# The forward substitution of a chunked delta rule: 30 small instructions per group, on GpSimd or on VectorE

## The chip, the core and the metric

One core of a Trainium2 chip runs the whole program in one launch. The metric is the device time of that launch in microseconds (us), median of several runs, lower is better. Engines: PE is TensorE (matmuls; PEld its weight loads), DVE is VectorE, ACT is ScalarE, POOL is GpSimd, SP is SyncE, which here issues nearly all DMAs.

## The reference

One step of a hybrid encoder layer over 1024 prompt tokens and 64 sample tokens, model width 1024, float32. Adaptive modulation and an RMS norm, one input projection whose columns feed four head groups of width 256 (a depthwise convolution, a gated delta rule, pooling, and a stick-breaking attention), concatenation, one output projection, then modulation, norm and a SwiGLU feed-forward layer. The change is in the gated delta rule, which works on chunks of 64 tokens; in each chunk a unit lower triangular system of 64 equations is solved, and the state S is carried from chunk to chunk:

```python
lmat = jnp.where(strict, jnp.einsum('nbhid,nbhjd->nbhij', kb, kc) * decay, 0.0)
sol = lax.linalg.triangular_solve(lmat + jnp.eye(CHUNK), rhs, left_side=True, lower=True, unit_diagonal=True)
...
v_new = u_i - jnp.einsum('bhcd,bhde->bhce', w_i, S)
o = jnp.einsum('bhcd,bhde->bhce', q_i, S) + jnp.einsum('bhij,bhje->bhie', attn_i, v_new)
S = S * gl[..., None, None] + jnp.einsum('bhcd,bhce->bhde', k_i, v_new)
```

## The kernel before, in words

The tokens are two halves: HA has 512 prompt tokens, HB 512 prompt and the 64 sample tokens. Each half goes through input projection, the four head groups, output projection and feed-forward layer; work of the two halves overlaps.

**Order.** The program is written with tiles and a scheduler. The scheduler decides the order of the instructions on every engine, from data dependences, its own estimate of durations and priorities; `tc.high_priority()` raises the priority of what is issued inside it. Each engine then executes its own list strictly in that order, so an instruction that waits holds up all that stand behind it on its engine. A change in one place can therefore change the order of distant work.

**Weights.** Every projection splits a float32 weight tile of 128x1024 in two parts, `whi` and the remainder `wlo`, so that three matmuls give nearly float32 accuracy. `load_w` does it, at high priority: SP loads `wraw`, ACT makes `whi`, DVE makes `wlo` (L123), each in two buffers. PE multiplies (`pg`, L138) only as fast as DVE delivers `wlo`.

**The delta rule.** `delta(h)` calls `dn_group` five times: groups 1 and 2 for HA, 3 and 4 for HB's prompt tokens (four chunks and 64 partitions each), group 5 for the sample tokens (one chunk, 16 partitions, state `S_s`). A group makes `nl`, the negated triangular matrix. Its 16x16 diagonal blocks are inverted by forward substitution, with one block per partition, which takes a change of layout through DRAM:

1. `nl` goes to DRAM (`nld`, two DMAs) and comes back as `fsn` (four DMAs), one block of 256 numbers per partition.
2. `fst` is a copy of `fsn` with 1 added on its diagonal, then 14 times a multiply into `fsu` and an add into `fst`: 30 instructions, each depending on the one before.
3. `fst` goes to DRAM (`xd`, four DMAs) and comes back as `X` (two DMAs).
4. PE transposes `X` (`pw_...<-cst,X`, called pw0 below), ACT copies it to `Y`, and PE and DVE (`W`, `Y`, `X`) combine blocks twice; then `pu`, `pwt`, the state update (`pvn`, `vn`, `pkv`), the norm (`oss`) and `pof`, `kbe` to DRAM for the output projection.

**Modulation of the sample tokens.** `ada_sample` loads 32 tiles `wads` of 512 KB into two buffers by SP; DVE reduces each with one custom instruction (L212). The two buffers are shared with tiles (`mixs`) that HB's output projection needs. `wadt` is the same for the prompt tokens.

**HB's output projection** starts when `mixs` stands: `mixt` loaded from DRAM into two buffers, split by ACT and DVE. After it PE works through HB's feed-forward layer to the end.

Of the kernel before, what the change touches and what calls it, by code (L numbers as in the profile page):

```python
# [11 lines left out]
ALU = mybir.AluOpType  # L12
# [47 lines left out]
def hybrid_encoder_kernel(ctx: ExitStack, tc: tile.TileContext, io):  # L60
    nc = tc.nc
# [57 lines left out]
    def copy_v(out, in_):  # L119
        nc.vector.tensor_copy(out=out, in_=in_)  # L120

    def tt(out, a, b, op):
        nc.vector.tensor_tensor(out=out, in0=a, in1=b, op=op)  # L123
# [4 lines left out]
    def ts(out, a, s1, s2, op0, op1=None):  # L128
        if op1 is None:
            nc.vector.tensor_scalar(out, a, s1, None, op0)  # L130
        else:
            nc.vector.tensor_scalar(out, a, s1, s2, op0, op1)

    def ptt(out, a, b, op):
        nc.gpsimd.tensor_tensor(out=out, in0=a, in1=b, op=op)  # L135
# [551 lines left out]
    def dn_group(h, feats, gate, D, ch0, nch, tok0, mtok0, S):  # L687
# [4 lines left out]
        def T4(tag, bufs=1):  # L692
            return dn.tile([P, 576], F32, tag=tag, name=tag)[:, 0:128 * NCH]
# [42 lines left out]
        tmp = T4("X")  # L736
# [35 lines left out]
        nx = 2 * nch  # L772
# [3 lines left out]
        N = dn.tile([64, 256], F32, tag="fsn", name="fsn")[0:8 * nx]  # L776
        T = dn.tile([64, 256], F32, tag="fst", name="fst")[0:8 * nx]
        tmp = dn.tile([64, 64], F32, tag="fsu", name="fsu")[0:8 * nx]
        for q in range(4):
            nc.sync.dma_start(out=N[2 * nx * q:2 * nx * (q + 1)].rearrange("p (i j) -> p i j", j=16),  # L780
                              in_=ext[q, :, :, :, q].rearrange("i h x j -> (h x) i j"))
        N3, T3 = N.rearrange("p (i j) -> p i j", j=16), T.rearrange("p (i j) -> p i j", j=16)
        nc.gpsimd.tensor_copy(out=T, in_=N)
        nc.gpsimd.tensor_scalar(T[:, 0:256:17], T[:, 0:256:17], 1.0, None, ALU.add)
        for k in range(1, 15):
            n = 15 - k
            u3 = tmp[:, 0:n * k].rearrange("p (i j) -> p i j", j=k)
            ptt(u3, N3[:, k + 1:16, k:k + 1].to_broadcast([8 * nx, n, k]), T3[:, k:k + 1, 0:k].to_broadcast([8 * nx, n, k]), ALU.mult)
            ptt(T3[:, k + 1:16, 0:k], T3[:, k + 1:16, 0:k], u3, ALU.add)
        for q in range(4):  # L790
            nc.sync.dma_start(out=ins[q, :, :, :, q].rearrange("i h x j -> (h x) i j"),
                              in_=T[2 * nx * q:2 * nx * (q + 1)].rearrange("p (i j) -> p i j", j=16))
# [26 lines left out]
        for c in range(nch):  # L819
            pv2 = PS("pvn")  # L820
            for pair in range(2):
                j = (pair * nch + c) * 64
# [9 lines left out]
            for pair in range(2):  # L832
                j = (pair * nch + c) * 64
# [19 lines left out]
    def delta(h):  # L853
        D = dn_decays(h)
        for b in range(2):
            feats, gate = dn_feats(h, 256 * b, 256)
            for g in range(4 // NCH):
                dn_group(h, feats, gate, D, 4 * b + NCH * g, NCH, 64 * NCH * g, 256 * b + 64 * NCH * g, S_p)
        if h.samp:
            feats, gate = dn_feats(h, 512, 64)  # L860
            dn_group(h, feats, gate, D, 8, 1, 0, 512, S_s)
            nc.sync.dma_start(out=io["dn_s"], in_=S_s)
            nc.sync.dma_start(out=io["dn_p"], in_=S_p)
# [491 lines left out]
```

## Time and profile before

| | before |
|---|---|
| median of 3 runs (range) | 1495.17 us (1493.13 to 1499.02) |
| the profiled execution | 1496.6 us |
| its span in the trace | 1494.5 us |
| PE busy | 1406.4 us (94%) |
| DVE busy | 1026.7 us (69%) |
| ACT busy | 662.7 us (44%) |
| POOL busy | 88.5 us (6%) |
| mean granted TensorE clock | 0.971 |

The span is what the trace covers from the first to the last instruction; the execution is 2.1 us longer. Busy shares are means over the span, and stages differ much. A granted clock of 1 is 2.4 GHz, and half of it is 1.2 GHz.

### The profile page before, as it was taken

Reading aid. Unit: us, or ns where it says so; the run is one execution under the profiler, and the core shown is the slowest. Engines: PE = TensorE matmul, PEld = TensorE weight load, DVE = VectorE, ACT = ScalarE, POOL = GpSimd, SP = SyncE. Lnnn points to the kernel's source line nnn. Section 1 sums busy time; section 2 is a strip of 40 time slices with the busy share of each in tenths; the row PEclk is TensorE's granted clock in tenths of the full one; section 3 lists DMA queues with packets and bytes.
Section 4 is the critical chain, followed back from the end, with each engine's and each line's share of the span. In section 5 each row is a group of like instructions: output and inputs, shape, how many; then the busy total and the mean of one; then the engine's idle time right before and its main releaser. Section 6 shows DMA issues by size and latency. Waiting matters only on the chain.

```text
span 1494.5 us, 24787 instructions
## 1 busy us (share of the span) xinstructions
PE 1406.4 (94%) x9824; PEld 1222.5 (82%) x9824; DVE 1026.7 (69%) x1816; ACT 662.7 (44%) x1191; POOL 88.5 (6%) x196
## 2 busy tenths in 40 slices
PE   7999899979988799799999899999899999999999
PEld 5777688857966577587778587889799999999998
DVE  8788798855798999856765887444755545444444
ACT  4467554745474468556765332222422222222221
POOL 0003000300003000400210000000000000000000
PEclk9999999979998899899999899999999999999999
DMA  8675555555753422533324786222322222222222
GB/s 310 239 229 144 193 166 162 165 167 172 256 174 101 141 75 80 151 109 101 94 84 119 246 285 210 99 85 85 113 99 81 80 81 85 85 86 85 86 79 98
DMA packets 106867, 205.42 MB, mean 137 GB/s; under 512 B 39360, under 2 KB 49024, under 8 KB 106752
## 3 DMA queue, kind: packets, MB, share of 16 engines
q1 hardware_dynamic: 99936, 193.36, 39.9%
q0 software_dynamic: 6816, 10.49, 3.1%
q8 instruction: 77, 1.26, 0.3%
q14 instruction: 38, 0.31, 0.1%
HBM read 175.57 MB, written 28.24 MB: 136 GB/s over the span
## 4 chain that ended last, share of the span: by engine, by line
PE 65%; DMA 13%; DVE 12%; issue 4%; POOL 3%; ACT 2%; SPq 1%; DVEq 0%; POOLq 0%; ACTq 0%
PE pg L138 55%; DMA wadt<-in_wadat_dram 3%; DMA wads<-in_wadat_dram 3%; DVE cy L126 2%; DVE wlo L123 2%; PE pk L138 2%; PE psC L141 1%; POOL fst L135 1%; POOL fsu L135 1%; DVE lo L126 1%; PE psO L141 1%; PE z L141 1%; DVE wads L212 1%; ACT whi L117 1%; DMA wraw<-in_wup_dram 1%
## 5 line engine op out<-in xcount | busy, mean ns | idle before, releaser
L138 PE MATMUL pg<-hi,whi 128*128 128x288 f32 (+1 forms) x1504 | 506.0, 337 | 13.7 <-ACT hi L114 5.0
L138 PE MATMUL pg<-hi,wlo 128*128 128x288 f32 (+1 forms) x1504 | 500.4, 333 | 6.6 <-DVE wlo L123 6.6
L138 PE MATMUL pg<-lo,whi 128*128 128x288 f32 (+1 forms) x1504 | 499.3, 333 | 2.2 <-DVE lo L126 1.6
L117 ACT ACTIVATE whi<-wraw 128x1024 fp32r<-128x1024 f32 (+2 forms) x192 | 199.6, 1041 | 475.5 <-PE pg L138 411.4
L138 PEld LDWEIGHTS pg<-hi,whi 128*128 128x128 f32 x1504 | 286.5, 191 | 43.3 <-ACT whi L117 6.2
L138 PEld LDWEIGHTS pg<-hi,wlo 128*128 128x128 f32 x1504 | 286.2, 190 | 33.2 <-DVE wlo L123 9.0
L138 PEld LDWEIGHTS pg<-lo,whi 128*128 128x128 f32 x1504 | 287.0, 191 | 27.7 <-issue 2.9
L123 DVE TENSOR_TENSOR wlo<-wraw,whi 128x1024 fp32r<-128x1024 f32 (+2 forms) x192 | 230.4, 1200 | 104.9 <-ACT whi L117 103.0
L138 PE MATMUL pg<-g,whi 128*128 128x288 f32 (+1 forms) x1056 | 252.0, 330 | 1.4 <-DVE xA L126 0.9
L138 PEld LDWEIGHTS pg<-g,whi 128*128 128x128 f32 x1056 | 177.4, 188 | 18.3 <-DVE xA L126 2.2
L138 PE MATMUL pg<-g,wlo 128*128 128x288 f32 (+1 forms) x528 | 171.8, 328 | 0.0
L126 DVE SCALAR_TENSOR_TENSOR xs<-pg,mod,xs 128x288 f32<-128x288 f32 (+2 forms) x288 | 106.5, 412 | 85.7 <-PE pg L138 82.5
L123 DVE TENSOR_TENSOR fa<-fa,pg 128x288 f32<-128x288 f32 (+1 forms) x66 | 35.0, 531 | 106.6 <-PE pg L138 102.9
L138 PEld LDWEIGHTS pg<-g,wlo 128*128 128x128 f32 x528 | 99.3, 188 | 7.4
L126 DVE SCALAR_TENSOR_TENSOR cy<-cvb,vec,cy 128x512 f32<-128x512 f32 (+1 forms) x120 | 93.4, 793 | 0.3
L126 DVE SCALAR_TENSOR_TENSOR xA<-pg,mod,xA 128x512 f32<-128x512 f32 x96 | 70.6, 746 | 22.1 <-PE pg L138 21.6
L212 DVE CUSTOM_DVE_ANT_0 wadt<-wadt,cb,vec 128x1024 f32<-128x1024 f32 x32 | 41.0, 1282 | 31.1 <-DMA wadt<-in_wadat_dram 31.0
L114 ACT ACTIVATE e<-e 128x512 f32<-128x512 f32 (+4 forms) x100 | 52.0, 520 | 0.7
L138 PE MATMUL pg<-mixs,whi 128*128 128x288 f32 x256 | 50.9, 295 | 0.0
L212 DVE CUSTOM_DVE_ANT_0 wads<-wads,cb,vec 128x1024 f32<-128x1024 f32 x32 | 40.9, 1281 | 11.1 <-DMA wads<-in_wadat_dram 11.0
L114 ACT ACTIVATE zs<-zs 128x512 f32<-128x512 f32 (+4 forms) x50 | 25.9, 517 | 47.3 <-DVE zs L123 47.2
L138 PEld LDWEIGHTS pg<-mixs,whi 128*128 128x128 f32 x256 | 41.0, 188 | 0.1
(296 smaller groups left out, 1811.2 us busy)
## 6 DMA issues: line engine op xcount, KB each, us to landing
wraw<-in_wgate_dram SPq DMA_DIRECT2D x44, 512.0 KB, 3.3
wraw<-in_wup_dram SPq DMA_DIRECT2D x44, 512.0 KB, 3.3
wraw<-in_wdown_dram SPq DMA_DIRECT2D x44, 512.0 KB, 3.3
wadt<-in_wadat_dram SPq DMA_DIRECT2D x32, 512.0 KB, 5.0
wads<-in_wadat_dram SPq DMA_DIRECT2D x32, 512.0 KB, 4.4
wraw<-in_wfm_dram SPq DMA_DIRECT2D x30, 512.0 KB, 3.6
wraw<-in_wout_dram SPq DMA_DIRECT2D x16, 512.0 KB, 3.8
xA<-in_xa_dram SPq DMA_DIRECT2D x16, 256.0 KB, 6.0
```

Of the source, the lines that this page charges most:

```text
L114: nc.scalar.activation(out, in_, func, bias=bias, scale=scale)
L117: nc.scalar.activation(out, in_, ACTF.Copy)
L123: nc.vector.tensor_tensor(out=out, in0=a, in1=b, op=op)
L126: nc.vector.scalar_tensor_tensor(out, a, s, b, op0, op1)
L135: nc.gpsimd.tensor_tensor(out=out, in0=a, in1=b, op=op)
L138: return nc.tensor.matmul(out, lhsT=lhsT, rhs=rhs, start=start, stop=stop)
L141: nc.tensor.matmul(out, lhsT=lhsT, rhs=rhs, start=start, stop=stop, skip_group_check=True)
L212: nc.vector.tensor_tensor_reduce(out=junk, in0=w, in1=cbt[g], scale=1.0, scalar=V("b_ada", col), op0=ALU.mult, op1=ALU.add, accum_out=mod[ ...
```

## The change

The copy, the added diagonal and the 28 steps of each of the five groups are issued to DVE instead of POOL, inside `tc.high_priority()`. Shapes, data and the DMAs around them are the same.

```diff
-        nc.gpsimd.tensor_copy(out=T, in_=N)
-        nc.gpsimd.tensor_scalar(T[:, 0:256:17], T[:, 0:256:17], 1.0, None, ALU.add)
-        for k in range(1, 15):
-            n = 15 - k
-            u3 = tmp[:, 0:n * k].rearrange("p (i j) -> p i j", j=k)
-            ptt(u3, N3[:, k + 1:16, k:k + 1].to_broadcast([8 * nx, n, k]), T3[:, k:k + 1, 0:k].to_broadcast([8 * nx, n, k]), ALU.mult)
-            ptt(T3[:, k + 1:16, 0:k], T3[:, k + 1:16, 0:k], u3, ALU.add)
+        with tc.high_priority():
+            copy_v(T, N)
+            ts(T[:, 0:256:17], T[:, 0:256:17], 1.0, None, ALU.add)
+            for k in range(1, 15):
+                n = 15 - k
+                u3 = tmp[:, 0:n * k].rearrange("p (i j) -> p i j", j=k)
+                tt(u3, N3[:, k + 1:16, k:k + 1].to_broadcast([8 * nx, n, k]), T3[:, k:k + 1, 0:k].to_broadcast([8 * nx, n, k]), ALU.mult)
+                tt(T3[:, k + 1:16, 0:k], T3[:, k + 1:16, 0:k], u3, ALU.add)
```

`ptt` is POOL's tensor-tensor instruction, `tt`, `ts` and `copy_v` are DVE's. What the scheduler makes of it is read from the order of instructions on the engines.

First, POOL in group 1 before, where steps of the substitution stand alone (the other groups read alike):

```order
L135 TENSOR_TENSOR fsu<-fsn,fst 64x26
L135 TENSOR_TENSOR fst<-fst,fsu 64x13x2
L135 TENSOR_TENSOR fsu<-fsn,fst 64x36
L135 TENSOR_TENSOR fst<-fst,fsu 64x12x3
L135 TENSOR_TENSOR fsu<-fsn,fst 64x44
L135 TENSOR_TENSOR fst<-fst,fsu 64x11x4
```

And DVE in group 3 now, where `dnf`, `dne` belong to the delta rule's features, `zs`, `sl`, `pl` to the attention and `cy` to the convolution:

```order
L123 TENSOR_TENSOR dnf_4852<-dnf_4852,dne 128x512
L123 TENSOR_TENSOR sl<-e,sh 128x384
L123 TENSOR_TENSOR pl<-zs,ph 128x256
L126 SCALAR_TENSOR_TENSOR dne<-dnf_4874,dne 128x512
L123 TENSOR_TENSOR fst<-fst,fsu 64x13x2
L123 TENSOR_TENSOR zs<-zs,psC 128x384
L123 TENSOR_TENSOR fsu<-fsn,fst 64x36
L123 TENSOR_TENSOR fst<-fst,fsu 64x12x3
L123 TENSOR_TENSOR fsu<-fsn,fst 64x44
L123 TENSOR_TENSOR cy_6720<-cy_6720,cvr 128x606
L123 TENSOR_TENSOR cy_6769<-cy_6769,cvr 128x606
L123 TENSOR_TENSOR fst<-fst,fsu 64x11x4
```

The steps moved to DVE, and they do not stand together there: between the first and the last of a group's 30 rows DVE has other rows, most in group 3, where there are 96.

Second, PE where group 5's `X` is used. Before, matmuls of the feed-forward layer (`pg`) and of the attention (`psC`, `z`) stand around pw0:

```order
L138 MATMUL pg<-hi_7283,whi 128x512
L138 MATMUL pg<-lo_7284,whi 128x512
L138 MATMUL pw_5497<-cst,X 64x64
L138 MATMUL pg<-hi_7283,wlo 128x512
L138 MATMUL pw_5497<-cst,X 64x64 x3
L141 MATMUL psC<-sl,u_r 128x512
L141 MATMUL z<-q_6266,k_6264 128x512 x2
```

Now the same place reads:

```order
L138 MATMUL pg<-g_8821,wlo 128x512
L138 MATMUL pw_5497<-cst,X 64x64 x4
L138 MATMUL pw<-Y,nl 64x64 x4
L138 MATMUL py<-W,X 64x64 x4
L138 MATMUL px<-X,W 64x64 x4
L138 MATMUL pw<-Y,nl 64x64 x4
L138 MATMUL py<-W,X 64x64 x4
L138 MATMUL pu<-vb,Y 64x64 x4
L138 MATMUL pwt<-Y,kbe 64x64 x4
L138 MATMUL pvn<-S_s,X 64x64
```

The group's matmuls moved next to each other, down to its `pof` (not shown), and behind work of HA's feed-forward layer that stood after them before.

Third, DVE at the same place. Before, the blocks are combined between other rows, and no `wads` row stands near:

```order
L123 TENSOR_TENSOR pl<-zs,ph 128x512
L123 TENSOR_TENSOR W<-pw,cst 128x128
L126 SCALAR_TENSOR_TENSOR fe<-fa,fe 128x512
L123 TENSOR_TENSOR sl<-e,sh 128x512
L123 TENSOR_TENSOR fa<-fa,fe 128x512
L123 TENSOR_TENSOR fa<-fa,pg 128x512
L123 TENSOR_TENSOR wlo<-wraw,whi 128x1024
L123 TENSOR_TENSOR Y<-Y,py 128x128
L123 TENSOR_TENSOR X<-X,px 128x128
```

Now the last rows of the substitution stand behind the last rows of `wads`, and the combination follows at once:

```order
L123 TENSOR_TENSOR fst<-fst,fsu 16x2x13
L212 ISA wads,mod<-wads,cb_154,vec 128x1024
L212 ISA mod 128x1
L123 TENSOR_TENSOR fsu<-fsn,fst 16x14
L123 TENSOR_TENSOR fst<-fst,fsu 16x14
L123 TENSOR_TENSOR W<-pw,cst 128x128
L123 TENSOR_TENSOR Y<-Y,py 128x128
L123 TENSOR_TENSOR X<-X,px 128x128
```

All 32 `wads` rows moved ahead of group 5's last step; before, the first of them stood behind group 5's `kbe`.

## Rows read from the trace of the kernel before

**Rows 1.** The page: engines, and DVE's busy tenths in 40 slices

```profile
PE 1406.4 (94%) x9824; PEld 1222.5 (82%) x9824; DVE 1026.7 (69%) x1816; ACT 662.7 (44%) x1191; POOL 88.5 (6%) x196
...
DVE  8788798855798999856765887444755545444444
```

**Rows 2.** Waits of PE: for what, us in total, times, longest

```profile
PE pw L138 <- DMA X<-xd: 26.8, 4, 9.7
PE pg L138 <- DVE wlo L123: 6.6, 7, 2.0
```

**Rows 3.** Timeline of PE, pw0 of groups 1 to 5, and matmuls after group 1's

```profile
156.53 0.30 PE L138 MATMUL pw<-cst,X 64*64 64x64 f32 x2 [2.97 <-DMA X<-xd]
...
160.62 0.63 PE L138 MATMUL pg<-hi,whi 128*128 128x512 f32 x1
...
161.43 0.39 PE L138 MATMUL pg<-hi,wlo 128*128 128x512 f32 x1
...
307.65 0.44 PE L138 MATMUL pw<-cst,X 64*64 64x64 f32 x2 [9.67 <-DMA X<-xd]
...
472.57 0.45 PE L138 MATMUL pw<-cst,X 64*64 64x64 f32 x2 [6.66 <-DMA X<-xd]
...
631.62 0.44 PE L138 MATMUL pw<-cst,X 64*64 64x64 f32 x2 [7.50 <-DMA X<-xd]
...
756.16 0.33 PE L138 MATMUL pw<-cst,X 64*64 64x64 f32 x2
```

**Rows 4.** Busy time by stretch: PE, PEld, DVE, ACT, POOL; then granted clock

```profile
0.00:400.00 400.00, 364.87 (x2858) 304.67 (x2859) 307.13 (x592) 219.01 (x444) 34.91 (x82) 0.96 0.63 198
400.00:627.00 227.00, 195.99 (x1379) 149.46 (x1377) 218.11 (x371) 144.09 (x270) 34.19 (x70) 0.95 0.43 128
627.00:740.00 113.00, 107.87 (x842) 86.01 (x843) 73.03 (x128) 69.72 (x145) 6.86 (x13) 0.96 0.34 103
...
819.00:925.00 106.00, 97.28 (x395) 75.86 (x395) 90.76 (x137) 36.14 (x55) 0.00 (x0) 0.94 0.78 256
925.00:1494.00 569.00, 561.35 (x3926) 543.67 (x3924) 288.96 (x518) 144.60 (x195) 0.00 (x0) 0.99 0.27 89
```

**Rows 5.** POOL's timeline, first and last row of group 1, last of group 5

```profile
134.57 0.79 POOL L783 COPY fst<-fsn 64x256 f32<-64x256 f32 x1
...
148.60 0.21 POOL L135 TENSOR_TENSOR fst<-fst,fsu 64x14 f32<-64x14 f32 x1
...
750.18 0.21 POOL L135 TENSOR_TENSOR fst<-fst,fsu 16x14 f32<-16x14 f32 x1
```

**Rows 6.** DVE's groups: shape and count, busy us and mean ns of one, idle before

```profile
L123 DVE TENSOR_TENSOR wlo<-wraw,whi 128x1024 fp32r<-128x1024 f32 x178 | 217.4, 1222 | 102.2 <-ACT whi L117 100.3 <-PE pl L138 0.5
L126 DVE SCALAR_TENSOR_TENSOR cy<-cvb,vec,cy 128x606 f32<-128x606 f32 x60 | 49.7, 842 | 0.0
L212 DVE CUSTOM_DVE_ANT_0 wads<-wads,cb,vec 128x1024 f32<-128x1024 f32 x32 | 40.9, 1281 | 11.1 <-DMA wads<-in_wadat_dram 11.0
L123 DVE TENSOR_TENSOR cvb<-cvb,cve 128x64 f32<-128x64 f32 x2 | 0.4, 216 | 0.0
L123 DVE TENSOR_TENSOR plo<-plo,plb 64x16 f32<-64x16 f32 x4 | 0.7, 167 | 0.1
L123 DVE TENSOR_TENSOR W<-pw,cst 128x128 f32<-128x128 f32 x2 | 0.6, 292 | 2.7 <-PE pw L138 2.7
```

**Rows 7.** DVE's timeline: two wlo, the first and the last wads

```profile
535.42 1.22 DVE L123 TENSOR_TENSOR wlo<-wraw,whi 128x1024 fp32r<-128x1024 f32 x1
...
737.63 1.22 DVE L123 TENSOR_TENSOR wlo<-wraw,whi 128x1024 fp32r<-128x1024 f32 x1
...
823.02 1.28 DVE L212 CUSTOM_DVE_ANT_0 wads<-wads,cb,vec 128x1024 f32<-128x1024 f32 x1
...
921.52 1.28 DVE L212 CUSTOM_DVE_ANT_0 wads<-wads,cb,vec 128x1024 f32<-128x1024 f32 x1
```

**Rows 8.** PE's timeline in group 5: one small batch of matmuls

```profile
762.07 0.45 PE L138 MATMUL pw<-Y,nl 64*64 64x64 f32 x8
```

## The prediction

> **What bounds the kernel now.** I read the page first. PE is busy 1406.4 of 1494.5 us, DVE 1026.7 and POOL only 88.5, but DVE's slices are uneven: eights and nines in the first half, fours and fives at the end [rows 1]. So I cut the span into stretches [rows 4]. From 400 to 627 us DVE is busy 218.1 of 227 us while PE has 31 us idle: DVE bounds there. After 925 us PE is busy 561 of 569 us: PE bounds to the end. Between them DVE has slack, except from 819 to 925 us, where the `wads` tiles pass (DVE 90.8 of 106 us, PE 97.3, clock 0.94).
>
> The waits of PE show what the chain of the delta rule costs: 26.8 us in four waits for `X` [rows 2]. The timeline gives them: 2.97, 9.67, 6.66 and 7.50 us in groups 1 to 4, none in group 5 [rows 3]. After each the clock is at half for some us: behind group 1's wait a 128x512 matmul takes 0.63 us at 160.62 and 0.39 from 161.43, four to five us after PE resumed [rows 3]. Taking 4 to 7 us at the halved level, 2 to 3.5 us lost each, the four waits cost about 10 us more.
>
> POOL needs 14.2 us for group 1, from 134.57 to 148.81 [rows 5]. In group 5 the last step ends at 750.39 [rows 5] and pw0 starts at 756.16 [rows 3]: 5.8 us for the way through DRAM, which the change leaves alone.
>
> **The change, part by part.** *The steps' own price.* DVE had no such instruction; the nearest rows are 0.167 us for 64x16 and 0.216 us for 128x64 [rows 6], and the steps have 14 to 56 numbers per partition, so 30 of them take 5.0 to 6.5 us, 25 to 32 us in five groups. Done in one piece they would save 8 to 9 us of the chain in each group. But the order shows that they are not in one piece. Between the first and last of group 3's rows stand 96 others, and pricing all rows between copy and last step with the mean of their form (1.22 for `wlo`, 0.84 for a `cy` row, 1.28 for `wads` [rows 6] and so on) gives 20, 45, 65, 30 and 44 us for the five groups, against 14.2 on POOL in group 1. The chain gets longer, and the scheduler has pushed pw0 back by 12 to 88 us of PE work to suit. What that does I work out in four terms, by what PE has lost (time less the full-clock price of the rows that PE has executed) at four places.
>
> *Term 1, up to the third gate tile of HA's feed-forward layer.* Its `wlo` starts at 535.4 us [rows 7]. Summing the orders by mean durations, DVE's rows up to it take 445.7 us before and 484.5 now: the steps of groups 1, 2 and most of 3, and attention, convolution and state rows that now come before it. PE's rows before its use take 360.1 and 361.4. Before, PE had lost 535.4 - 360.1 = 175.3 us there, and DVE had stood idle 89.7. Of DVE's idle time the waits for `X` in groups 1 and 2 go (12.6 us and 4 of clock): their pw0 now stands behind a `wlo` that DVE makes about when the last step is done. I leave 3 us for what remains. That gives 484.5 + 89.7 - 16.6 + 3 = 560.6 at the tile, and PE has lost 560.6 - 361.4 = 199: **+24 us**. Bounds: +10, if DVE finds other gaps filled, and +32, if each of three groups also holds DVE for 3 us at the copy, which waits for its four DMAs with `wlo` rows queued behind it.
>
> *Term 2, from there to a feed-forward tile at 737.6 us* [rows 7]. Before, PE's rows up to it sum to 528.8, so it had lost 208.8: 33.5 us in this part, of which 10 to DVE until 627, 10.5 to group 4's wait for `X` and its clock, 13 to smaller things. Now DVE's lead over PE's needs has come back: by 627 us its lag, rows of DVE less rows of PE, has fallen from 123 at the gate tile to 103. So the first goes, group 4's wait shrinks to 3 us at most, and I give the small ones half. That leaves about 7: **-27 us**, bounds -33 and -12. Up to here the change is about even, -3 us.
>
> *Term 3, `wads`.* Before, 32 tiles took from 823.02 to 921.52 [rows 7], 98.5 us, 3.08 each, with waits of DVE for their DMA of 11.0 us [rows 6]: two buffers of 512 KB set the pace. They lay over PE rows of 85 us. Now the first stands 42 us of PE work earlier, the last before group 5's last step, and PE's rows between are 67 us. If the pace stays, PE loses 31 us there instead of the 18 to 22 it lost before: **+9 us**, bounds 0 and +13.
>
> *Term 4, group 5's end.* Before, it lay under feed-forward and attention matmuls and no wait stood at pw0 [rows 3]. Now PE has nothing between its small batches, and an `xA` row that stands on DVE a few places ahead of the last steps needs PE's last filling matmuls. So all is bare: 5.8 us for `X`; then 11 hops on DVE and ACT of 0.29 us (a 128x128 row takes 0.292 [rows 6]) with gaps of 0.1 to 0.2, 5.5 us; ten batches of 0.45 us [rows 8], PE's own work, but at half the clock, 4.5 us more; 2 us until the clock is back; and 4 us (0 to 8) because the next `wlo` stands behind five `mixs` rows. **+22 us**, bounds +12 (clock kept, no `mixs`) and +28.
>
> Nothing else moves: from HB's output projection on, the orders of PE are the same, and POOL's freed time is worth nothing, since it was busy 88.5 us in all.
>
> *Sum.* 1496.6 (the profiled execution) + 24 - 27 + 9 + 22 = 1524.6. The median of the runs is 1.4 us below that execution: about **1523 us**, 1.9% slower.
>
> **The rivals.** *Faster, because the chain gets shorter.* DVE does a step in 0.17 to 0.22 us, where POOL averaged 14.2 / 30 = 0.47. If the steps go through with little between them, as they would where the rows between wait for nothing and DVE has slack, the four waits (26.8 us) and their clock (10 us) vanish, group 5 stays under cover, and term 1 costs nothing: 1495.2 - 37 = 1458. For it: the waits are there, and in groups 1 and 5 DVE is not full. Against it: the order, in which the rows between are fixed, and 96 of them lie in the stretch where DVE is busy 96% [rows 4]. It decides if term 1 is under 5 us and pw0 of group 5 does not wait. The Trainium skill ("GPSIMD Engine Reference", section 4.1, Engine selection) says to put elementwise adds and multiplies on VectorE and not on GpSimd, which it finds about twice as slow for two inputs; by that rule the change should win. The trace agrees on the price of one instruction, 0.47 against 0.17 to 0.22; but the rule prices an engine by itself and not a place in another engine's queue. 10%.
>
> *About even.* Term 1 is near its low bound, because DVE's own gaps (it was idle 93 of the first 400 us [rows 4]) take up the new rows, and term 4 is near 12 as the clock stays up: 1496.6 + 10 - 27 + 5 + 12 = 1496.6, or 1495 on the median's scale. For it: terms 1 and 2 nearly cancel anyway. Against it: 400 to 627 us has no slack, and the bare stretch on PE stands in the order. 16%.
>
> *Slower still.* Each step on DVE depends on the one before, and the copy waits for DMAs at the head of DVE's queue; where the rows between are `wads` or `xA`, it waits for the DMA or for PE as well. With term 1 at +32, term 3 at +13 and term 4 at +28 the time is 1496.6 + 32 - 27 + 13 + 28 = 1542.6, or 1541. 12%.
>
> The forecast itself, 1508 to 1537, holds the remaining 62%.
>
> **How the numbers follow.** The predicted time is that of the four terms, 1523. The range leaves out the faster rival and the tail of the slower one: 1495 to 1541. A difference under 0.5%, 7.5 us, can't be told from none with runs that lie 5.9 us apart. Faster by more: the first rival and a part of the second, 0.11. Within 0.5%: most of the second, 0.13. Slower: forecast and third rival, with what the second leaves, 0.76.
>
> **What would show each step.** In the profile of the changed kernel: DVE about 25 to 32 us busier and POOL nearly empty; waits of PE for `X` in groups 1 to 4 down to a few us, with the longest now in group 5, 6 us or more, and small waits after it in the matmuls of group 5 for DVE and ACT; DVE full from some 380 to 560 us, and PE waiting for `wlo` there; a stretch with the `wads` rows ahead of group 5's `X` in which DVE waits for their DMA; and from HB's output projection on the old times, shifted by one constant. I am wrong if pw0 of group 5 starts without a wait, if the gate tile's `wlo` starts before 545 us, or if the steps take much more than 0.2 us each on DVE.

## The result, and the profile after

The changed kernel takes **1508.24 us** (median; 1507.65 to 1509.81), the one before, run on the same chip, 1495.88: ratio 1.0077, interval 1.0058 to 1.0095. It is slower, by 12 us where the prediction said 28: the direction holds and the size does not. The profiled execution took 1508.54 us, its span is 1506.8.

The page after, engines and DVE's slices, answers to [rows 1]:

```profile
PE 1409.3 (94%) x9824; PEld 1224.4 (81%) x9824; DVE 1045.7 (69%) x1966; ACT 666.2 (44%) x1191; POOL 24.2 (2%) x46
...
DVE  8788898975999995796587744444755445444444
```

DVE has the 150 new instructions and is 19.0 us busier; POOL has lost 64.3 us. The waits of PE after (for what, us in total, times, longest) answer to [rows 2]:

```profile
PE pw L138 <- DMA X<-xd: 12.4, 1, 12.4
PE psC L141 <- DVE zs L123: 12.2, 6, 5.9
PE pg L138 <- DVE xA L126: 8.6, 6, 3.9
```

All four waits for `X` are gone and a single one has come, in group 5. The next two rows are waits for DVE. PE's timeline at group 5's pw0, then busy time (PE, PEld, DVE, ACT, POOL) and granted clock of the 20 us about and behind it:

```profile
865.09 1.22 PE L138 MATMUL pw<-cst,X 64*64 64x64 f32 x8 [12.38 <-DMA X<-xd]
```

```profile
860.00:870.00 10.00, 3.63 (x40) 2.72 (x40) 1.51 (x8) 0.28 (x1) 0.00 (x0) 0.50 0.04 10
870.00:880.00 10.00, 6.42 (x68) 5.26 (x69) 3.16 (x8) 3.29 (x9) 0.00 (x0) 0.50 0.15 42
```

PE sits idle from 852.7 to 865.1, and the granted clock is 0.50, the lower level of 1.2 GHz, for the 20 us shown. DVE's timeline says why `X` is late:

```profile
856.36 1.26 DVE L212 CUSTOM_DVE_ANT_0 wads<-wads,cb,vec 128x1024 f32<-128x1024 f32 x1
...
857.56 0.17 DVE L123 TENSOR_TENSOR fst<-fst,fsu 16x26 f32<-16x26 f32 x1
858.83 1.29 DVE L212 CUSTOM_DVE_ANT_0 wads<-wads,cb,vec 128x1024 f32<-128x1024 f32 x1 [1.10 <-DMA wads<-in_wadat_dram]
...
860.23 0.16 DVE L123 TENSOR_TENSOR fst<-fst,fsu 16x14 f32<-16x14 f32 x1
```

Steps of 0.16 us wait their turn among `wads` rows that wait for their own DMA. From the last step to pw0 another 4.7 us pass through DRAM.

To account for the 12 us I cut both spans at the same rows of DVE: where it starts the gate tile's `wlo` and the feed-forward `wlo` [rows 7], and a `wlo` behind the `wads`. Before:

```profile
0.00:400.60 400.60, 365.46 (x2862) 305.27 (x2863) 307.74 (x594) 219.57 (x446) 34.91 (x82) 0.96 0.63 198
400.60:535.40 134.80, 109.23 (x801) 82.76 (x799) 128.35 (x212) 73.25 (x133) 17.83 (x36) 0.92 0.44 136
535.40:737.60 202.20, 191.62 (x1405) 150.16 (x1406) 160.15 (x283) 138.99 (x278) 21.07 (x44) 0.97 0.37 110
737.60:923.30 185.70, 176.98 (x828) 139.23 (x828) 139.83 (x212) 85.53 (x141) 14.64 (x36) 0.96 0.58 185
923.30:1494.50 571.20, 563.05 (x3934) 545.06 (x3932) 290.66 (x520) 145.37 (x197) 0.00 (x0) 0.99 0.27 89
```

After, the same five pieces:

```profile
0.00:370.90 370.90, 345.77 (x2623) 292.08 (x2624) 308.85 (x628) 212.40 (x423) 10.19 (x22) 0.97 0.69 215
370.90:532.80 161.90, 131.66 (x799) 96.99 (x798) 160.34 (x296) 99.01 (x189) 3.36 (x6) 0.85 0.42 123
532.80:717.80 185.00, 184.73 (x1408) 146.91 (x1408) 144.54 (x275) 132.92 (x251) 9.94 (x17) 1.00 0.39 110
717.80:934.70 216.90, 183.36 (x1068) 142.79 (x1065) 142.59 (x254) 77.54 (x136) 0.76 (x1) 0.92 0.49 160
934.70:1506.80 572.10, 563.81 (x3937) 545.63 (x3935) 289.37 (x517) 144.34 (x195) 0.00 (x0) 0.99 0.26 89
```

The first piece (cut at one `wlo` of the merge weights on both sides) is 29.7 us shorter, the second 27.1 longer with DVE busy 160.34 of 161.90, the third 17.2 shorter with PE busy throughout, the fourth 31.2 longer, the last 0.9 longer. These add up to 12.3, the difference of the spans.

PE's rows in a piece are not the same, though. Up to the first cut it has executed 2623 instead of 2862, mostly because group 2's state update (`pu` to `pof`) now stands behind it, and in the fourth piece it has 1068 instead of 828, most of the added ones group 4's. Of the first piece's 29.7 us, 10.0 are idle time of PE and 19.7 busy time; of the fourth's 31.2, 24.8 are idle and 6.4 busy.

### The profile page after: what moved, and what is told of

It reads as the page before. It is cut to its first block, busy times and chain, and to the rows that moved or that the text cites. A ratio compares the mean times of both kernels' runs of the same rounds, so it can differ in the third digit from the quotient of the medians.

```text
span 1506.8 us, 24778 instructions
## 1 busy us (share of the span) xinstructions
PE 1409.3 (94%) x9824; PEld 1224.4 (81%) x9824; DVE 1045.7 (69%) x1966; ACT 666.2 (44%) x1191; POOL 24.2 (2%) x46
## 4 chain that ended last, share of the span: by engine, by line
PE 67%; DVE 15%; DMA 10%; issue 3%; ACT 3%; SPq 1%; DVEq 0%; ACTq 0%
PE pg L138 57%; DMA wads<-in_wadat_dram 3%; DVE cy L126 2%; DVE wlo L123 2%; PE psC L141 2%; DMA wadt<-in_wadat_dram 1%; DVE wads L212 1%; DVE dnf L126 1%; PE psO L141 1%; PE pv L138 1%; PE z L141 1%; DVE junk L212 1%; DVE xA L126 1%; PE pw L138 1%; DVE wadt L212 1%
## 5 line engine op out<-in xcount | busy, mean ns | idle before, releaser
L126 DVE SCALAR_TENSOR_TENSOR xA<-pg,mod,xA 128x512 f32<-128x512 f32 x96 | 71.0, 746 | 15.6 <-PE pg L138 14.9
L114 ACT ACTIVATE fa<-pg 128x288 f32<-128x288 f32 (+1 forms) x52 | 22.3, 428 | 40.9 <-PE pg L138 40.9
```

The source lines that it names most:

```text
L114: nc.scalar.activation(out, in_, func, bias=bias, scale=scale)
L126: nc.vector.scalar_tensor_tensor(out, a, s, b, op0, op1)
```

## The experiments

The prediction's theory, *place*: a step on DVE costs its place in DVE's queue; group 5's bare end and the full stretch lose more than the vanished waits give. Its rivals: *price*, the steps' own time on DVE counts, wherever they stand; *length*, the chain's duration is what matters and a shorter one wins; *packing*, what counts is how the rows around the steps come to stand, the `wads` above all.

Each time stands beside that of the kernel before, run on the same chip. Pieces and leads come from one profiled execution of a kernel, and executions of one kernel lie up to 13 us apart, so a few us between two profiles show little.

### Which group costs what

The kernels of this part differ in which groups' steps run on DVE. In the first all but group 5 do:

```diff
+        if samp_g:
+            nc.gpsimd.tensor_copy(out=T, in_=N)
...
+                ptt(T3[:, k + 1:16, 0:k], T3[:, k + 1:16, 0:k], u3, ALU.add)
+        else:
             with tc.high_priority():
                 copy_v(T, N)
```

> Groups 1 to 4 on DVE as in the change, group 5's 30 instructions back on POOL. The orders are those of the changed kernel up to group 5; then pw0 of group 5 stands 18 us of PE work ahead of its pof instead of 3, with feed-forward matmuls between. Theory A (the loss lies in group 5's bare end): the 12.4 us wait for X in group 5 and most of the small waits behind it go, so the time falls by 12 to 20 us below the changed kernel, to 1488 to 1496, at or below the kernel before. Theory B (the loss comes from the 32 wads tiles being squeezed into an earlier place, wherever group 5's steps run): the tiles stay where they are, PE waits the same time for wlo behind them, and the time stays at 1503 or more.

1501.62 us against 1498.12, ratio 1.0026 (1.0010 to 1.0042). The piece that holds the `wads` and group 5:

```profile
717.90:924.50 206.60, 184.94 (x1070) 143.35 (x1065) 138.78 (x225) 77.13 (x136) 14.92 (x31) 0.94 0.53 168
```

206.6 us, between 185.7 before and 216.9 after. So by the profiles some 10 of the 31 us belong to group 5's steps (by the medians, 12.4 us against 3.5 above the kernel before, 9) and 21 to what groups 1 to 4 have changed in the order of that piece.

From here on the condition chooses DVE, with POOL's block under the else. Group 5 alone:

```diff
-        with tc.high_priority():
+        if samp_g:
+            with tc.high_priority():
```

> The reverse: groups 1 to 4 on POOL as before, only group 5 on DVE. The order keeps the wads tiles behind group 5, and 38 us of PE work between its pw0 and pof. Theory A in the form that DVE steps in group 5 are bad by themselves: 1503 to 1510. Theory A in the form that only the place counts, where group 5 has nothing left on PE to stand under: the same as before, 1493 to 1498, with waits for X of 26 us in groups 1 to 4.

1496.69 against 1498.12, 0.9993 (0.9974 to 1.0011): no difference. The same 30 rows cost about 10 us in the one order and nothing in the other. *Price* by itself doesn't hold.

Groups 1 and 2, then 3 and 4:

```diff
-        if samp_g:
+        if h.name == 'A':
```

> Only HA's groups 1 and 2 on DVE, groups 3 to 5 on POOL. If the gain of the change up to 400 us (the profile shows the kernel there 30 us earlier than before) belongs to groups 1 and 2 alone, and groups 3 and 4 only push DVE further behind, then this keeps most of it: the waits for X in groups 3 and 4 (14 us) stay, and the time is 1475 to 1488. If the early gain is only borrowed, because the same DVE rows come later in the stretch where DVE is full (the prediction's first term), nothing is left: 1492 to 1500.

```diff
-        if h.name == 'A':
+        if h.name == 'B' and not samp_g:
```

> Only HB's groups 3 and 4 on DVE, the others on POOL. The order spreads group 3's 30 rows over 121 us of DVE work and brings group 5's pw0 to pof to 3 us of PE work again. Theory A: the bare end of group 5 (about 35 us in the changed kernel) without the gain of groups 1 and 2 makes it the slowest, 1512 to 1525. If the steps in groups 3 and 4 are what helps, since their waits for X are 14 us: 1490 or less.

1493.66 (0.9972, interval 0.9953 to 0.9991) and 1534.34 (1.0252, 1.0219 to 1.0285). The first half is slightly faster, and the second alone costs more than the whole change: 36 us. Its loss shows about group 5, whose steps are on POOL here:

```profile
830.00:930.00 100.00, 65.70 (x342) 49.16 (x341) 62.28 (x111) 26.36 (x49) 16.25 (x30) 0.78 0.55 176
```

PE is idle 34 of 100 us at a clock of 0.78, and DVE isn't full either (62.28): the order has left PE nothing to do beside group 5's chain. That is the bare end that *place* speaks of, made by moving other groups' steps.

Groups 1 and 4, then 1, 2 and 4:

```diff
-        if h.name == 'B' and not samp_g:
+        if (h.name == 'A' and ch0 == 0) or (h.name == 'B' and ch0 == 4):
```

> Only groups 1 and 4 on DVE, 2, 3 and 5 on POOL. The order leaves the wads tiles and group 5 nearly where they were, and pw0 of groups 1 and 4 stands 12 and 25 us of PE work later. If each group's wait for X goes where its steps move to DVE and nothing is taken back: the waits of groups 1 and 4 (10.5 us) and 5 us of clock, 1480 to 1487. If it is taken back by DVE or by other waits: 1492 to 1500.

```diff
-        if (h.name == 'A' and ch0 == 0) or (h.name == 'B' and ch0 == 4):
+        if (h.name == 'A' and ch0 == 0) or (h.name == 'A' and ch0 == 4) or (h.name == 'B' and ch0 == 4):
```

> Groups 1, 2 and 4 on DVE, 3 and 5 on POOL: the changed kernel's early part without its group 3, whose 30 rows stand among 96 others, and with group 5 under cover (40 us of PE work from pw0 to pof). If group 3 on DVE is what gave the early gain back: 1475 to 1486. If the gain is lost because DVE is full there in any case, as with groups 1 and 2 alone (1494): 1490 to 1498. If the earlier place of wads costs here too: above 1498.

1493.76 (0.9974, 0.9953 to 0.9994) and 1494.18 (0.9985, 0.9962 to 1.0009) against 1496.75: small gains at best. The first is 16.4 us ahead of the kernel before at the feed-forward tile and has 3.3 us of it left behind the `wads`.

One group at a time, and 2 with 4:

```diff
-        if (h.name == 'A' and ch0 == 0) or (h.name == 'B' and ch0 == 4):
+        if (h.name == 'A' and ch0 == 0):
```

> Only group 1 on DVE. Open is why DVE's idle time ahead of the feed-forward layer fell by 36 us where 14 were forecast. If it falls because everything behind a late X waits with it (PE's small batches, attention, wadt), group 1 alone frees 12 to 18 us of DVE's idle time up to the wfm tile at 401 us, though its wait for X was only 3 us, and that tile starts 12 to 18 us earlier; if DVE's idle time falls by the wait and its clock alone, 5 us. The total: 1488 to 1497, as part of it is given back in the full stretch.

```diff
-        if (h.name == 'A' and ch0 == 0):
+        if ch0 == 4 and h.name == 'A':
```

> Only group 2 on DVE. By the same theory its wait of 9.7 us frees 12 to 20 us of DVE's idle time up to the wfm tile at 401 us; by the wait and its clock alone, 12 us. As its steps stand among 45 us of DVE work just ahead of the full stretch, the total is 1492 to 1500.

```diff
-        if ch0 == 4 and h.name == 'A':
+        if (h.name == 'B' and ch0 == 4):
```

> Only group 4 on DVE, whose steps come where DVE is about to have slack again (from 627 us). Its wait for X (7.5 us and 3 of clock) goes and nothing has to be paid in the full stretch: 1484 to 1490. If wads and group 5 behind it take it back: 1493 to 1498.

```diff
-        if (h.name == 'B' and ch0 == 4):
+        if (h.name == 'A' and ch0 == 4) or (h.name == 'B' and ch0 == 4):
```

> Groups 2 and 4 on DVE. If the groups' effects add: the two results before this together, some 1480 to 1492. If the stage of wads takes any gain back that comes from ahead of it: 1493 to 1498.

Against 1495.66: group 1 alone **1488.41**, 0.9945 (0.9923 to 0.9968), the fastest kernel with all the work in it, half a per cent ahead of the kernel before; group 2 alone 1501.06, 1.0046 (1.0022 to 1.0070); group 4 alone 1500.23, 1.0036 (1.0019 to 1.0054); 2 and 4 together 1499.00, 1.0023 (1.0009 to 1.0038). The totals don't add. DVE has room where group 1's steps are: the kernel before, from 130 to 160 us about group 1 and from 280 to 310 about group 2, has DVE busy 16.28 and 26.40 of 30 us:

```profile
130.00:160.00 30.00, 27.03 (x113) 21.14 (x114) 16.28 (x31) 13.60 (x24) 13.09 (x32) 0.97 0.55 163
280.00:310.00 30.00, 20.33 (x183) 18.43 (x183) 26.40 (x51) 16.20 (x36) 12.52 (x30) 0.86 0.37 110
```

That fits the one gain without showing its cause: PE's waits for `X` sum to 29.0 us with group 1 alone, more than the 26.8 before, and the profiled execution, 1493.63, is the slowest of its nine.

The first piece does add. Up to the `wlo` where it ends, with group 1 and with group 2 alone:

```profile
0.00:383.60 383.60, 356.09 (x2790) 299.58 (x2791) 306.82 (x602) 215.17 (x428) 25.30 (x52) 0.95 0.65 206
```

```profile
0.00:385.30 385.30, 356.00 (x2737) 298.52 (x2738) 307.59 (x600) 214.59 (x428) 22.42 (x52) 0.96 0.64 207
```

DVE's idle time there is 92.9 us before, 76.8 and 77.7 here and 62.0 after: 16.1 and 15.2 less, 31.3 together, and 30.9 with both. Each group by itself gives DVE 15 to 16 us. Here too PE has executed fewer rows at the cut, 72 and 125.

### What the chain and the steps are worth

Three of 14 step pairs on POOL, the other eleven left out, nothing moved to DVE:

```diff
-        for k in range(1, 15):
+        for k in range(1, 4):
```

> The kernel before, with only the first 3 of the 14 pairs of steps on POOL (8 instructions instead of 30, some 10 us less per group); the rest of the substitution is left out. It shows what the chain's length is worth by itself. As the prediction priced it, the four waits for X (26.8 us) and their half clock (10 us) go: 1458 to 1468. If DVE's full stretch from 400 to 627 us takes most of it back, as it did with the changed kernel's early gain: 1478 to 1490.

1482.99 against 1496.75, 0.9910 (0.9882 to 0.9938). The waits for `X` sum to 16.6 us; the gate tile is 26.0 us earlier than before, the feed-forward tile 21.7, the `wlo` behind the `wads` 13.8. *Length* is right that a shorter chain wins. The 37 us that the waits and their clock were put at were not to be had here, since 16.6 of the 26.8 us of waits are left; for the 10.2 that went, the same price gives an estimate of 14 us, and the end shows 14. Up to the first piece's end:

```profile
0.00:380.80 380.80, 360.06 (x2856) 301.78 (x2857) 305.76 (x577) 217.35 (x436) 16.54 (x38) 0.97 0.65 209
```

DVE is idle 75.0 us there, 17.9 less than before, though it got no new rows, and up to the gate tile (509.4, DVE busy 433.27) 76.1 against 99.3. The waits of groups 1 and 2 for `X` shrank by 8.9 us only, from 12.6 to 3.7. So the shorter chain gives DVE about twice as much as PE's waits for `X` alone show. With nearly the same rows (2856 against 2862) the 19.8 us by which the piece is shorter are, on PE, 8.9 of this wait, 5.5 of other idle time and 5.4 of busy time, at a granted clock of 0.97 instead of 0.96.

POOL does the steps as before, and DVE 31 additional rows of 64x16 in each group, which nobody uses:

```diff
+        gh = dn.tile([64, 16], F32, tag="gsu", name="gsu")[0:8 * nx]
+        with tc.high_priority():
+            copy_v(gh, N[:, 0:16])
+            for k in range(1, 16):
+                tt(gh, N[:, 16 * k:16 * k + 16], gh, ALU.mult)
+                tt(gh, N[:, 16 * k:16 * k + 16], gh, ALU.add)
```

> The kernel before, with the substitution on POOL as it was, and besides 31 dependent DVE instructions of 64x16 per group (about 0.16 us each, 5 us per group, 25 us in all, at high priority) on a small tile that nobody reads: DVE's extra work without the change of the chain. Theory A (the step of the prediction that failed is that DVE's extra rows cost PE time; DVE's gaps take them up): 1495 to 1502. Theory of the prediction (from 400 to 627 us DVE is full, so that what groups 1 to 4 add ahead of it is paid): 10 to 20 us more than before, 1507 to 1516.

1527.81, 1.0206 (1.0164 to 1.0248). As a price of DVE's rows this is not clean: the waits for `X` grew from 26.8 to 42.5 us, because POOL's steps took longer (group 1 from 14.2 to 19.6 us). After those 16 us, and some 5 that I estimate for their clock, about 10 of the 31 us remain for DVE's rows and their order. Some rows of POOL, and of DVE beside them:

```profile
293.86 0.36 POOL L135 TENSOR_TENSOR fst<-fst,fsu 64x56 f32<-64x56 f32 x1
294.30 6.33 POOL L135 TENSOR_TENSOR fsu<-fsn,fst 64x56 f32<-64x56 f32 x1
300.71 0.29 POOL L135 TENSOR_TENSOR fst<-fst,fsu 64x56 f32<-64x56 f32 x1
```

```profile
294.58 1.27 DVE L212 CUSTOM_DVE_ANT_0 wadt<-wadt,cb,vec 128x1024 f32<-128x1024 f32 x1
...
299.28 1.20 DVE L123 TENSOR_TENSOR wlo<-wraw,whi 128x1024 fp32r<-128x1024 f32 x1
300.41 0.67 DVE L123 TENSOR_TENSOR zs<-zs,psC 128x512 f32<-128x512 f32 x1
```

One POOL step takes 6.33 us, its neighbours of the same size 0.29 and 0.36, and for its whole length DVE has no gap.

### The `wads`

Thirty-two loads of `wads` replaced by two (the same two tiles are used again), in the kernel before and in the changed one:

```diff
+        two = []
         for j in range(32):
-            t = sb.tile([P, 1024], F32, tag=("k2", "q2")[j % 2], name="wads")
-            nc.sync.dma_start(out=t, in_=io["wadat"][j])
-            ada_dve(t, 16 + j, (1,))
+            if j < 2:
+                two.append(sb.tile([P, 1024], F32, tag=("k2", "q2")[j % 2], name="wads"))
+                nc.sync.dma_start(out=two[j], in_=io["wadat"][j])
+            ada_dve(two[j % 2], 16 + j, (1,))
```

> The kernel before with only 2 of the 32 wads tiles loaded; DVE reduces these two again and again, so that its work stays and 30 loads of 512 KB are left out (the sample tokens' second modulation is then not the reference's). If the pace of the loads costs PE what it lost from 819 to 923 us (8.7 us idle and 6.8 us of clock): 1481 to 1487. If DVE's reductions are what holds PE up there: 1493 or more.

> The changed kernel with the same loads left out (2 of 32 tiles loaded). Its lead of 13 us at 730 us is lost and 29 us of loss come in from there to 890 us. If that is the pace of wads ahead of group 5's last steps: 1478 to 1490, level with or below the other kernel without these loads. If it is group 5's bare end by itself (X, hops and half clock, about 20 us): 1495 to 1503, and 10 us or more above the other kernel without these loads.

Against 1494.85 the kernel before takes 1506.81 without these loads, 1.0083 (1.0055 to 1.0112): slower. The changed one takes 1499.53, 1.0039 (1.0018 to 1.0059), 7 us less than its counterpart, and its wait for `X` in group 5 is gone. In the kernel before the reductions no longer wait for loads and now stand close together on DVE; the stretch between two `wlo` without the loads, which now holds all 32 reductions, and between the same two with the loads, where 16 of them stand:

```profile
816.50:878.70 62.20, 44.77 (x167) 32.80 (x167) 61.72 (x101) 22.29 (x38) 0.00 (x0) 0.89 0.28 94
```

```profile
819.00:871.20 52.20, 45.26 (x177) 33.82 (x177) 43.64 (x68) 22.30 (x39) 0.00 (x0) 0.90 0.78 257
```

DVE is busy 61.72 of 62.2 us, and PE, with nearly the same work, takes 10 us longer. Without the loads the changed kernel is the faster one of the two. That doesn't clear the loads: without them the changed kernel gains some 0.4% (1.0077 to 1.0039), and the kernel before loses 0.8% as its reductions close up.

All loads, but three buffers:

```diff
-            t = sb.tile([P, 1024], F32, tag=("k2", "q2")[j % 2], name="wads")
+            t = sb.tile([P, 1024], F32, tag=("k2", "q2", "v2")[j % 3], name="wads")
```

> The kernel before with three buffers for wads instead of two (the third is the tile v2, free there). If two buffers set the pace of 3.08 us per tile: PE's loss from 819 to 923 us shrinks, 1484 to 1492. If the loads are held by the DMA queues themselves: as before, 1493 to 1498.

> The changed kernel with three buffers for wads. In its order group 5's steps are spread over 30 instead of 44 us of DVE work. If the pace of wads is the cause of its loss: 1488 to 1498, at or below the kernel before. If group 5's bare end is: 1502 to 1508.

1506.90 before, 1.0077 (1.0050 to 1.0103), and 1502.07 after, 1.0049 (1.0028 to 1.0069). Again the kernel before loses 12 us and the changed kernel gains, so that it is 5 us ahead. In both pairs the changed kernel is ahead, so the sign of the change hangs on what is done about the `wads`. That speaks for *packing*, but both edits also change the scheduler's order, and most of the turn is the loss of the kernel before; that the packing alone decides is not shown.

## Why the prediction was right in direction and wrong in size

**Term 1, +24 us up to the gate tile: the step that failed.** The tile starts at 532.84 us, not 560.6 and below the 545 that was named as refuting it. DVE's rows up to it went from 436.1 to 469.2 us, +33.1 where the forecast had +38.8. The mistake lies in "of DVE's idle time the waits for `X` in groups 1 and 2 go", with 13.6 us net of the 3 left over: DVE's idle time fell by 35.7, from 99.3 to 63.6. The steps give DVE back 15 to 16 us for each of groups 1 and 2, by the two kernels with one group each. I had read PE's wait for `X` and its clock as all of DVE's idle time that hangs on the steps. The cut chain shows that there is more: 8.9 us less of this wait went with 17.9 less idle time of DVE.

But the changed kernel doesn't shorten the chain. On DVE group 1's steps take 22.5 us from the copy to the last step, where POOL took 14.2, and `X` is used 10 us later than before in group 1 and 37 in group 2 ([rows 3]: 156.53 and 307.65), without a wait:

```profile
166.63 1.15 PE L138 MATMUL pw<-cst,X 64*64 64x64 f32 x32
...
344.18 0.33 PE L138 MATMUL pw<-cst,X 64*64 64x64 f32 x2
```

The waits went because the order has put other work of PE ahead of `X`. The same order puts group 2's state update behind the first cut. The forecast counted the waits in that order and not what else it moves; how the 35.7 us divide between them is not shown. DVE's own waits up to the first piece's end say where it lay before:

```profile
DVE wadt L212 <- DMA wadt<-in_wadat_dram: 25.6, 16, 6.2
DVE cve L126 <- ACT cve L114: 9.2, 1, 9.2
```

and after:

```profile
DVE wadt L212 <- DMA wadt<-in_wadat_dram: 17.3, 9, 4.6
...
DVE cve L126 <- ACT cve L114: 1.9, 1, 1.9
```

These two alone give 15.6 us, and neither names `X`; with group 1 alone the wait for `wadt` is still 23.9 us, so they are not the same in each kernel. The full stretch itself came as forecast: from 370.9 to 532.8 us DVE has 1.6 us free, and the 29.7 us won ahead of it shrink to 2.6. What PE waits for there is `zs` (11.9 of the 12.2 us above), not `wlo` as I had said.

**Term 2, -27 us to the feed-forward tile: right in kind, measured -17.2.** PE is busy 184.73 of 185.00 us there, so all loss is gone. I had put the loss of before at 33.5; it was about 17, the 202.2 us of this piece less 185 of PE's work. I take the reason to be that PE's rows were summed from the order with the small float32 matmuls counted once, where the trace shows each as two (eight for the four of pw0), so that PE's work here came out as 528.8 - 360.1 = 168.7 us instead of 185.

**Terms 3 and 4, +9 and +22 us: measured +31.2 together**, in part by luck. 6.4 us of it are busy time of PE, which has group 4's state update in this piece now. And term 3 doesn't follow from its own rows: 98.5 us over 85 of PE's work are a loss of 13.5 us before, not 18 to 22, and the term would have been +18. The wait for `X` is 12.4 us, not 5.8, and the half clock lasts 20 us and more. The `wads` rows are among the steps and wait for their DMA, as said. That the group's steps themselves account for only 10 of the 31 us was not in the terms: the kernel with group 5 on POOL has the rest as well.

**The rest.** After HB's output projection nothing moved: +0.9 us. The chains' lengths on DVE, 22.5, 48.2, 63.2, 29.5 and 48.0 us in groups 1 to 5, came out as forecast (20, 45, 65, 30 and 44). A step on DVE takes 0.16 to 0.21 us, as priced, but DVE is only 19.0 us busier instead of 25 to 32 (below). Against +24, -27 and +31 the pieces miss by -26.6, +9.8 and +0.2, and the tail by +0.9: -15.7, the difference between 28 and 12.3.

**The rivals.** Faster by a shorter chain: on DVE the chain got longer. Where it was cut short on POOL, 14 us came out at the end, with 16.6 us of the waits left. About even expected term 1 near its low bound of +10; it came out below that, but term 4 was not near its own, and 12 us were left. Slower still needed term 1 at +32. The sentence of the Trainium skill ("GPSIMD Engine Reference", section 4.1, Engine selection) that elementwise work belongs on VectorE is borne out for group 1 alone (-0.55%) and not for groups 3 and 4 (+2.5%). The price of one instruction was as it says; the total hung on which groups moved.

**What stays open.** Where the lead is given back is shown: all kernels that are ahead at the feed-forward tile, the changed one and eleven others, lose a third of the lead or more by the end of the `wads` (16.4 to 3.3 us with groups 1 and 4, 21.7 to 13.8 with the cut chain; group 4 alone turns 6.9 ahead into 6.8 behind). It is not one-sided, though: of the five that are behind there, three catch up, groups 1 and 2 from 10.2 us behind to 0.8. So this piece evens out much of what lies ahead of it, and a lead there is not yet a gain; why, no run shows. Why the one order leaves PE bare beside group 5 and another does not was read from the orders only; no run held the order and changed the engine alone.

## What to carry to other kernels

Before moving small steps to another in-order engine, look at the idle time that the engine has at each place, group by group, and don't take the consumer's wait as the whole price of the chain, nor its end as a sign that the chain got shorter. Here the group where DVE was half idle gave 7 us by itself; all five together cost 12. Where a scheduler places the rows, follow the lead to a point behind the next crowded stage before counting it as won, since here that stage took back a third of it or more, and fewer loads, or a third buffer for them, made the otherwise unchanged kernel 0.8% slower.

## What was not expected of the hardware

**Small rows on DVE overlap.** DVE's timeline after, at the start of group 1's steps and in their middle:

```profile
135.86 0.17 DVE L130 TENSOR_SCALAR fst<-fst 64x16 f32<-64x16 f32 x1
135.94 0.16 DVE L123 TENSOR_TENSOR fsu<-fsn,fst 64x14 f32<-64x14 f32 x1
136.03 0.68 DVE L123 TENSOR_TENSOR dnf<-dnf,dne 128x512 f32<-128x512 f32 x1
...
148.26 0.20 DVE L123 TENSOR_TENSOR fsu<-fsn,fst 64x56 f32<-64x56 f32 x1
148.50 0.21 DVE L123 TENSOR_TENSOR fst<-fst,fsu 64x56 f32<-64x56 f32 x1
```

The row of the diagonal and the first step last 0.16 to 0.17 us each, but what follows them starts 0.08 and 0.09 us after they do. Two dependent steps in a row start 0.24 us apart. So 150 rows of 0.19 us, 29 us by their durations, made DVE only 19.0 us busier.

**A step on POOL stretched about twentyfold while DVE ran without a gap**: 6.33 us for a 64x56 step against 0.29 to 0.36, in the kernel with the additional rows above. The neighbours ran beside rows of DVE as well (the one at 300.71 us beside `zs`), so a busy DVE alone doesn't do it. The Trainium skill ("GPSIMD Engine Reference", section 1, Specifications) says that POOL shares its interfaces to SBUF with VectorE and contends with instructions that have two inputs there. The long step fits that, and the rows don't show it to be the cause.
